# Seventh product on a copy in another bank, o's sums behind the gate, and the first two units side by side, in a fp32 decoder step

## The chip, the cores and the metric

The kernel runs on one core of a Trainium2 chip. The metric is device time in microseconds (us) for one execution; lower is better. The engines of a core work side by side and wait for one another through semaphores: TensorE (PE) multiplies matrices into PSUM banks, VectorE (DVE) and ScalarE (ACT) work on elements, GpSimd (POOL) does small work and starts stores, SyncE (SP) starts loads. Each engine runs its instructions in the order of its own queue.

## The reference

The program is one inference step of a decoder: 1024 prompt tokens and 8 decode tokens, model width 2048, everything in fp32. Two layers are computed, layer A (a pooling mixer) and layer B (sliding-window attention). Cut to the products:

```python
def pool_layer(x, ...):              # layer A
    z = x @ w_in                     # 2048 -> 4096
    u, gate = z[..., :D_POOL], z[..., D_POOL:]
    d, new_state = multiscale_pool(u, prefix, pos)   # windows 2, 4, 8, 16, minus u
    d = einsum('btgc,gce->btge', d, w_grp) * scale
    y = (d * silu(gate)) @ w_out
    return layer_norm(ALPHA * x + y, g_ln, b_ln), new_state

k, v = shared_kv(h)                  # 4 heads of 64, once, from layer A's output

def attn_layer(x, ...):              # layer B
    z = x @ w_in                     # 2048 -> 4096: queries and gate
    o = attn_core(rope(q), kb, vb)   # window of 128, a sink per head
    y = (o * silu(gate)) @ w_out
    return layer_norm(ALPHA * x + y, g_ln, b_ln)
```

The outputs are the result for prompt and decode tokens, and the new states of the pooling and of the keys and values.

## The kernel before

**Tokens and phases.** Chunk 0 holds 512 tokens; chunk 1 holds the other 512 and the 8 decode tokens, 520 columns. The program goes through ten phases in order: `ai` (input product of layer A) for chunk 0 in two parts and chunk 1, `ao` (output product of A) for chunks 0 and 1, `bi` (input product of B, with the attention beside it) for chunk 0 in two parts and chunk 1, `bo` (output product of B) for chunks 0 and 1. Activations and weights carry the letters x, g, h, o for the inputs of `ai`, `ao`, `bi`, `bo`, and `wia`, `woa`, `wib`, `wob` for the weights.

**An fp32 product from three.** Each weight tile and each activation tile is split into a high part, rounded to the matrix unit's format by a cast on ScalarE (L474 for weights, L752 for activations), and a low part, the rest, by a subtraction on VectorE (L489 and L761). For each of 8 slices of the inner dimension TensorE does three matmuls: high·high, high·low (the activation's low part), low·high (the weight's low part).

**Units and pairs.** The first part of `ai` and of `bi` is done in plain units (`unit`, L669 to L671): one 128 x 512 output from 16 slices, about 11.1 us. Everywhere else `pair` and `both` compute two output tiles at once by Strassen's scheme in Winograd's form (`seven`, L641 to L643): seven products of half the size, in the order 0, 2, 1, 5, 3, 4, 6 (another order for the first two pairs of most phases, which run interleaved in `both`). The products gather in PSUM banks a, b, c:

- product 0 goes to bank a; ScalarE writes its negative into bank b (`p0`, L582);
- product 2 goes to c, and is copied out (`p2`); product 1 is added in b, and copied out (`p1`);
- product 5 is added in a, and a is copied out (`p5`); product 3 is added in b, and VectorE subtracts product 2's copy from b into an output (`p3`, L602);
- product 4 is added in c, and VectorE subtracts from c (`p4`, L607); product 6 is added in b, and ScalarE copies b out (`p6`, L614).

The string that says this is `names = "abcbcab"`: the bank of product 0, 1, 2 and so on. Product 6 thus may start only when L602 has read b. With the `c11` and `split` forms a few pairs are treated in another way. Banks come from three pools (`psD`, a ring) and, in phases where `wide` holds, from four more (`psW`, used for a and c). A function such as `p3` is not issued at once: it is put into `posts`, and the next product's `begin` issues it first.

**Streams.** The weights come as a list of entries, in the order of use. `begin` (the start of each product) loads up to 7 entries ahead (SP, `load1`, L273), casts 4 ahead and makes low parts 3 ahead; in `bi` of chunk 1, where fewer than 4 whole slots are free, one less of each. The activations' tiles come in the same manner by `x_load`, `x_cast` and `x_make`. All of these live in 53 slots of on-chip memory (`NSLOT`); an entry whose slot is not free is loaded later. `end` (the end of each product) runs one late addition, the events that `at(n, go)` has put n products ahead, a step of the activations, and a step of the side work: generators such as `t_gen`, the layer norms, the sums of weights.

**Sums for Strassen's scheme.** Sums of weight quadrants are made once, on VectorE, and kept in DRAM: L279 in the first groups (four additions for each pair of rows, `late` in `plain_pair`, one at the end of each step), L332 and its neighbours later. Sums of activation quadrants are made by `t_ops` (four VectorE operations, L809 to L812), stored to `Td`, and loaded again by `x_load`; for x of chunk 0 `t_first` (L719 to L722) makes them from tiles still on chip.

**The attention of chunk 1 and o.** The attention runs beside the pairs of `bi`, tile by tile (t = 0 to 15): scores, exponentials (L1778), transposes, values, then `gate` (L1828), which writes a tile of o and stores it. For chunk 0 the sums of o are made right there from two neighbouring tiles (t − 1 and t). For chunk 1 the tile is freed at once; a side generator, `t_gen(("o", 1))`, added 18 steps into `bo` of chunk 0, later loads the pairs of tiles back (eight loads of 520 KB), sums them (eight calls of `t_ops`) and stores the sums. The decode tokens' own attention is done in small steps (L1919 to L1962) and stored into the last 8 columns of o.

**The start.** `start` issues the first loads, 512 KB each, in the order weight a, four tiles of x, weight, two of x, weight, two of x; then casts and low parts in the order of use. Unit 0 runs over all 16 slices, then unit 1 over the same tiles of x.

PE, VectorE and ScalarE keep the order of the source (`in_order`).

Of the kernel before, what the change touches and what calls it, by code (L numbers as in the profile page):

```python
# [9 lines left out]
F32 = mybir.dt.float32  # L10
# [52 lines left out]
ENGINES = (mybir.EngineType.PE, mybir.EngineType.DVE, mybir.EngineType.Activation)  # L63
NSLOT = 53
KEEP0 = 1

# [5 lines left out]

LATE = (2, 3)
X_KEEP = 5
X_AGE = 3
# [106 lines left out]
class Kern:  # L182
    def __init__(self, ctx, tc, io):
# [25 lines left out]
        self.ahead = 7, 4, 3  # L209
        dr = lambda n, s: dram.tile(s, F32, tag=n, name=n)  # L210
        self.Td, self.act, self.l_sq, self.l_sh = {}, {}, {}, {}
        for c, (_, T) in enumerate(CHUNKS):
# [56 lines left out]

    def load1(self, s, k, src):  # L270
# [15 lines left out]
    def plain_pair(self, name, q):  # L286

        a11, a12, a21, a22 = self.quads(name, q)
        ws = self.ws[name][q]
        s = {}  # L290
        ent = lambda k, src, after: Entry([self.load1(s, k, src)], [], lambda: s[k], after)
# [6 lines left out]
        return [  # L298
            ent("a", a11, []),
            ent("d", a12, []),  # L300
            ent("b", a21, []),
            ent("c", a22, [lambda: self.late.extend(late)]),
        ]

    def lone(self, src):
# [259 lines left out]
    def seven(self, c, z0, z1, after, c11=None, split=False, own=None):  # L565
# [4 lines left out]
        TH = T // 2  # L570
        B, o = {}, {}

        def out(i):
# [6 lines left out]
        def p0():  # L580
            B["b"] = self.psD()
            nc.scalar.mul(B["b"][:, :TH], B["a"][:, :TH], -1.0)  # L582
            if split:
                nc.scalar.copy(out(0)[:, :TH], B["a"][:, :TH])
# [15 lines left out]

        def p3():
            nc.vector.tensor_sub(out(1)[:, TH:T], B["b"][:, :TH], o["s"].a[:, :TH])  # L602
            if split:
                nc.scalar.copy(out(1)[:, :TH], B["b"][:, :TH])
# [5 lines left out]
        def p6():  # L610
            if split:
                nc.vector.tensor_add(out(1)[:, :TH], B["f"][:, :TH], out(1)[:, :TH])
            else:
                nc.scalar.copy(out(1)[:, :TH], B["b"][:, :TH])  # L614

        posts = {0: p0, 1: p1, 2: p2, 3: p3, 4: p4, 5: p5, 6: p6}
        names = "abcbcef" if split else "abcbcab"

        def run(idx):
# [11 lines left out]
            if new and own is not None and bank in "ac":  # L631
                B[bank] = own() if bank == "a" else B["a"]
            elif new:
                B[bank] = self.psW() if bank in "ac" else self.psD()
            ps = B[bank]
# [19 lines left out]
    def unit(self, done):  # L655
# [3 lines left out]
        for par in range(2):  # L659
            w = self.begin()  # L660
            wh, wl = (s.r for s in w)
            for k in range(8):
# [16 lines left out]
                if k in (3, 7):  # L679
                    self.end()  # L680


    def x_begin(self, n):
# [42 lines left out]
    def x_load(self):  # L726
        i, g = k = self.xl.pop(0)
        key = self.xkey
        T = CHUNKS[key[1]][1]
        TH = T // 2  # L730
        s = self.mem.full()
        if self.xseven:
            t = s.v(4, TH)
            if i in (0, 4, 5):
                k0, h = {0: (0, 0), 4: (1, 1), 5: (1, 0)}[i]
                src = self.act[key][:, 8 * g + k0 : 8 * g + 8 : 2, h * TH : (h + 1) * TH]
            else:
                src = self.Td[key][:, 4 * g : 4 * g + 4, {1: 0, 2: 1, 3: 2, 6: 3}[i], :]
        else:
            t = s.v(2, T)  # L740
            src = self.act[key][:, 4 * g + i : 4 * g + 4 : 2, :]
        self.nc.sync.dma_start(t, src)
        self.xraw[k] = s, self.i

    def x_cast(self, k):
        if k not in self.xraw:
            assert k == self.xl[0]
            self.x_load()
        s, _ = self.xraw.pop(k)
        n = 4 * (CHUNKS[self.xkey[1]][1] // 2) if self.xseven else 2 * TP  # L750
        h = self.mem.full()
        self.nc.scalar.copy(h.r[:, :n], s.a[:, :n])  # L752
        self.xhi[k] = s, h, n, self.i
# [361 lines left out]
    def phase_ai(self, c, gs, nxt):  # L1115
# [4 lines left out]
        for g in gs:  # L1120
            ext = es = None
            if T > TP:
                es = self.mem.half()
                ext = es.a[:, :512].rearrange("p (i b w) -> p i b w", i=4, b=NDEC)
                nc.sync.dma_start(ext, io["st"][:, 4 * g : 4 * g + 4])
            dd, sg = {}, {}
            for i in range(4):
                if not self.strassen:

                    def done(ps, i=i):  # L1130
                        U = self.mem.full()
                        nc.scalar.copy(U.a[:, NST : NST + T], ps[:])
                        self.at(1, lambda: self.pool_tile(c, 4 * g + i, U, None, dd))

                    self.unit(done)
                elif i % 2 == 0:
# [154 lines left out]
    def phase_end(self, c, xs, x_in, pre, acc, gc, bc, out):  # L1291
# [16 lines left out]
        A2 = slice(0, 2 * P)  # L1308
        four = self.small(NK * 4, 1)
        f3 = four[:].rearrange("p (k t) -> p k t", k=NK)  # L1310
        b2 = lambda x: x[:, None, :].to_broadcast([P, 2, TH])
# [416 lines left out]
    def attend(self, c, t, at, s1, s2, late=False):  # L1728
# [96 lines left out]
        def gate():  # L1825
# [6 lines left out]
            if c == 1:  # L1832
                self.ao.pop((c, t)).free(True)
            elif t % 2:
                e = self.ao.pop((c, t - 1))
                self.t_ops(e.a[:, :TP], a.a[:, :TP], self.Td["o", c], t // 2, T // 2)
                e.free(True)
                self.ao.pop((c, t)).free(True)
            if j == 1 or t == 15 or self.sg.get((c, t + 1), (None,))[0] is not z:
# [9 lines left out]
        self.product(at + s1 + s2, 1, values)  # L1849
        self.at(at + s1 + s2 + 1, gate)  # L1850

    def gate_done(self, c, t0, s, n):
# [29 lines left out]
    def decode(self, c, pr):  # L1882
# [77 lines left out]
        def s9():  # L1960
            a3 = self.sgd[pr][:]
            nc.vector.scalar_tensor_tensor(  # L1962
                a3, x["p"][:, :64].rearrange("p (b t) -> p t b", t=8), 0.5, a3,
                op0=ALU.mult, op1=ALU.mult,
            )
            nc.sync.dma_start(self.act["o", c][:, 8 * pr : 8 * pr + 8, TP:], a3)
            x["v"].free()
            W.free()
# [84 lines left out]
    def start(self):  # L2053
# [5 lines left out]
        self.x0, self.pre, self.held = {}, {}, set()  # L2059
        self.load_to(1)  # L2060
        for n in range(8):
            self.x_load()
            if n in (3, 5):
                self.load_to(n // 2 + 1)
# [3 lines left out]
        self.prep_to(1)  # L2068
        for n in range(8):
            self.x_make()  # L2070
            if n == 3:
                self.prep_to(2)
        for j in range(4):
# [7 lines left out]
    def run(self):  # L2081
# [15 lines left out]
        for n, (kind, c, part) in enumerate(PHASES):  # L2097
# [213 lines left out]
```

## Time and profile before

| | |
|---|---|
| median of 3 runs | 2367.22 us (2366.88 to 2370.61) |
| profiled execution | 2367.62 us |
| its span | 2365.9 us |
| TensorE busy | 2326.4 us, 98% |
| VectorE busy | 1923.5 us, 81% |
| ScalarE busy | 1342.2 us, 57% |
| GpSimd busy | 201.5 us, 9% |
| DMA | 669.18 MB, mean 283 GB/s |
| first matmul | 7.96 us after the span's start |

Times in rows count from the start of the span. The span covers the instructions; the execution's time has 1.7 us around it. A name before `<-` is what an instruction writes, those behind it are what it reads: `m` is a slot, `pD` a bank of PSUM of a product, `x1` the number of instructions. A bracket at the end of a row tells how long the engine had been idle before, and which instruction ended that. In a list of waits the line in front is the one that waited, the line behind the arrow the one that released it.

### The profile page before, as it was taken

How to read it: one execution, taken by the hardware profiler on the slowest of the kernel's cores; microseconds unless marked ns; L12 is line 12 of the kernel's file. 1: busy time of each engine (PE TensorE's matmuls, PEld its weight loads, DVE VectorE, ACT ScalarE, POOL GpSimd, SP SyncE). 2: the span in 40 equal slices, each digit the busy share in tenths (PEclk: the TensorE clock that was granted, in tenths of full speed). 3: DMA queues.
4: the chain of work that ended last, by engine and by line, in shares of the span. 5: the costliest groups of instructions: out<-in, count | busy, mean ns of one | idle time of the engine just before them, and what ended most of it. 6: DMA issues, size and time to landing. Idle time of an engine off the chain costs nothing. (4 is left out here: it accounts for less than half of the span.)

```text
span 2365.9 us, 46542 instructions
## 1 busy us (share of the span) xinstructions
PE 2326.4 (98%) x18424; PEld 2219.4 (94%) x18424; DVE 1923.5 (81%) x2385; ACT 1342.2 (57%) x2429; POOL 201.5 (9%) x379
## 2 busy tenths in 40 slices
PE   8999999999999999999999999999999999999997
PEld 6899999999999999998778899999999999999997
DVE  8787998776878878868888888887777768888887
ACT  4444446544536547554554656685666667546556
POOL 0111110001000000000111111100000000000000
PEclk9999999999999999999999999999999999999999
DMA  8678789889889989989888766788787768699785
GB/s 294 215 244 303 274 291 349 308 308 315 286 278 365 331 270 324 334 314 330 282 324 322 258 230 224 238 297 275 232 259 221 222 193 298 227 353 371 259 302 194
DMA packets 252059, 669.18 MB, mean 283 GB/s; under 512 B 25760, under 2 KB 106560, under 8 KB 251840
## 3 DMA queue, kind: packets, MB, share of 16 engines
q1 hardware_dynamic: 206368, 501.14, 64.0%
q0 software_dynamic: 45472, 165.07, 17.9%
q8 instruction: 144, 2.36, 0.4%
q14 instruction: 75, 0.61, 0.1%
HBM read 471.01 MB, written 185.59 MB: 278 GB/s over the span
## 5 line engine op out<-in xcount | busy, mean ns | idle before, releaser
L641 PE MATMUL pD<-m,m 128*128 128x260 f32 (+1 forms) x4752 | 1346.9, 283 | 9.9 <-DVE m L602 3.7
L643 PE MATMUL pD<-m,m 128*128 128x260 f32 (+1 forms) x4752 | 1340.5, 282 | 4.5 <-DVE m L489 4.5
L642 PE MATMUL pD<-m,m 128*128 128x260 f32 (+1 forms) x4752 | 1340.3, 282 | 0.0
L641 PEld LDWEIGHTS pD<-m,m 128*128 128x128 f32 x4752 | 896.0, 189 | 21.0 <-issue 10.2
L643 PEld LDWEIGHTS pD<-m,m 128*128 128x128 f32 x4752 | 896.7, 189 | 6.0 <-DVE m L489 6.0
L642 PEld LDWEIGHTS pD<-m,m 128*128 128x128 f32 x4752 | 896.3, 189 | 0.5
L489 DVE TENSOR_TENSOR m<-m,m 128x1024 fp32r<-128x1024 f32 x674 | 814.1, 1219 | 96.1 <-ACT m L474 58.3
L474 ACT CAST m<-m 128x1024 fp32r<-128x1024 f32 x674 | 701.6, 1048 | 305.2 <-DVE m L332 71.3
L669 PE MATMUL pD<-m,m 128*128 128x512 f32 x448 | 179.7, 401 | 8.0 <-ACT m L752 8.0
L670 PE MATMUL pD<-m,m 128*128 128x512 f32 x448 | 177.2, 396 | 0.5 <-DVE m L761 0.5
L671 PE MATMUL pD<-m,m 128*128 128x512 f32 x448 | 177.2, 396 | 0.0
L761 DVE TENSOR_TENSOR m<-m,m 128x1024 fp32r<-128x1024 f32 (+1 forms) x120 | 146.9, 1225 | 7.2 <-ACT m L752 5.7
L614 ACT COPY m<-pD 128x260 f32<-128x260 f32 (+1 forms) x83 | 31.0, 373 | 188.2 <-PE pD L643 188.1
L752 ACT CAST m<-m 128x1024 fp32r<-128x1024 f32 (+1 forms) x120 | 125.7, 1052 | 14.2 <-PE pD L670 5.2
L669 PEld LDWEIGHTS pD<-m,m 128*128 128x128 f32 x448 | 84.7, 189 | 29.9 <-ACT m L752 8.0
L332 DVE TENSOR_TENSOR m<-m,m 128x1024 f32<-128x1024 f32 x88 | 107.6, 1222 | 5.9 <-DMA m<-in_wia 4.2
L670 PEld LDWEIGHTS pD<-m,m 128*128 128x128 f32 x448 | 84.8, 189 | 20.4 <-DVE m L761 1.6
L671 PEld LDWEIGHTS pD<-m,m 128*128 128x128 f32 x448 | 84.6, 189 | 19.8
L602 DVE TENSOR_TENSOR m<-pD,m 128x260 f32<-128x260 f32 (+1 forms) x86 | 36.4, 424 | 81.9 <-PE pD L643 78.6
L1778 ACT ACTIVATE m<-m,sm 128x128 f32<-128x128 f32 x256 | 99.2, 390 | 0.0
L1071 PE MATMUL pD<-m,m 128*128 128x260 f32 (+1 forms) x528 | 91.5, 323 | 0.0
L607 DVE TENSOR_TENSOR m<-pD,m 128x260 f32<-128x260 f32 (+1 forms) x84 | 35.6, 424 | 64.2 <-PE pD L643 64.0
(243 smaller groups left out, 2167.3 us busy)
## 6 DMA issues: line engine op xcount, KB each, us to landing
m<-in_wia SPq DMA_DIRECT2D x124, 512.0 KB
m<-in_wib SPq DMA_DIRECT2D x120, 512.0 KB
swia<-m POOLq DMA_DIRECT2D x64, 512.0 KB, 4.9
m<-swia SPq DMA_DIRECT2D x64, 512.0 KB
m<-swoa SPq DMA_DIRECT2D x64, 512.0 KB
swib<-m POOLq DMA_DIRECT2D x64, 512.0 KB, 5.3
m<-swib SPq DMA_DIRECT2D x64, 512.0 KB
m<-swob SPq DMA_DIRECT2D x56, 512.0 KB
```

Source lines behind the costliest of these rows:

```text
L332: self.nc.vector.tensor_add(s[out].a[:, :1024], s[x].a[:, :1024], s[y].a[:, :1024])
L474: self.nc.scalar.copy(hi.r[:, :1024], self.stream[self.cast].src().a[:, :1024])
L489: self.nc.vector.tensor_sub(lo.r[:, :1024], s.src().a[:, :1024], hi.a[:, :1024])
L641: nc.tensor.matmul(ps[:, :TH], wh[:, s], h, start=new and k == 0, stop=False, skip_group_check=on)
L642: nc.tensor.matmul(ps[:, :TH], wh[:, s], l, start=False, stop=False, skip_group_check=on)
L643: nc.tensor.matmul(ps[:, :TH], wl[:, s], h, start=False, stop=k == 7, skip_group_check=on)
L669: nc.tensor.matmul(ps[:], wh[:, s], h, start=par == 0 and k == 0, stop=False)
L670: nc.tensor.matmul(ps[:], wh[:, s], l, start=False, stop=False)
L671: nc.tensor.matmul(ps[:], wl[:, s], h, start=False, stop=par == 1 and k == 7)
L752: self.nc.scalar.copy(h.r[:, :n], s.a[:, :n])
L761: self.nc.vector.tensor_sub(l.r[:, :n], s.a[:, :n], h.a[:, :n])
L1778: nc.scalar.activation(x["s3"][:, i, :], x["s3"][:, i, :], AF.Exp, bias=nm[:, i : i + 1], scale=0.125, accum_out=rs[:, i : i + 1],)
```

## The change

Three things are changed.

1. *Seventh product.* In pairs that are neither `split` nor the second of two interleaved ones (`turned`, 73 pairs), `p3` first copies bank b to bank a on ScalarE, from PSUM to PSUM; product 6 is added in a, and `p6` copies a out. VectorE's subtraction still reads b. Where the phase is not `wide`, a and b change places from pair to pair among the first two pools (`flip`), and c has the third.
2. *o's sums.* For chunk 1 the gate keeps the tiles of o; three steps after the gate of each odd t, `t_ops` sums tiles t − 1 and t over all 520 columns, with zeros in the decode columns. The decode tokens' columns are kept in a small tile (`oa`); `o_dec` sums them apart, once for each half of the heads, into `otd`, and `x_cast` puts them into the loaded tiles before the cast. The generator in `bo` is gone.
3. *The start.* Seventeen dummy matmuls on zeros are issued first. The first two weights and the first two tiles of x come in transfers of 256 KB with casts and subtractions of 512 columns. `first_units` runs unit 0 and unit 1 side by side, tile of x by tile of x, so that each tile feeds twelve matmuls; a few dummies are put between the first ones. The order of the first four weights is a, b, d, c. The small constants are loaded behind the fifth weight.

```diff
-            self.nc.sync.dma_start(s[k].a[:, :1024], src)
+            for a, b in cuts:
+                self.nc.sync.dma_start(s[k].a[:, a:b], src[:, a:b])
...
+        turned = own is None and not split
+        three = None
+        if turned and not self.wide:
+            self.flip = 1 - self.flip
+            three = {"a": self.flip, "b": 1 - self.flip, "c": 2}
...
         def p3():
+            if turned:
+                nc.scalar.copy(B["a"][:, :TH], B["b"][:, :TH])
             nc.vector.tensor_sub(out(1)[:, TH:T], B["b"][:, :TH], o["s"].a[:, :TH])
...
-                nc.scalar.copy(out(1)[:, :TH], B["b"][:, :TH])
+                nc.scalar.copy(out(1)[:, :TH], B["a" if turned else "b"][:, :TH])
...
-        names = "abcbcef" if split else "abcbcab"
+        names = "abcbcef" if split else "abcbcaa" if turned else "abcbcab"
...
+    def first_units(self, dones):
+        nc = self.nc
+        banks = [self.psD() for _ in dones]
+        for par in range(2):
+            ws = {}
+            for n, (u, j) in enumerate((u, j) for j in range(4) for u in range(2)):
...
+                for i in range(2):
+                    k = 2 * j + i
...
+                    nc.tensor.matmul(banks[u][:], wh[:, s], h, start=par == 0 and k == 0, stop=False)
+                    if par == 0 and n == 0:
+                        self.idle(FILL[i])
+                    nc.tensor.matmul(banks[u][:], wh[:, s], l, start=False, stop=False)
+                    nc.tensor.matmul(banks[u][:], wl[:, s], h, start=False, stop=par == 1 and k == 7)
...
             if c == 1:
-                self.ao.pop((c, t)).free(True)
-            elif t % 2:
+                nc.gpsimd.memset(a.a[:, TP:T], 0.0)
+                nc.gpsimd.tensor_copy(self.oa[:, t, :], a.a[:, THM - NDEC : THM])
+                self.o_dec(t // 8)
+            if t % 2:
                 e = self.ao.pop((c, t - 1))
...
+                def sums():
+                    self.t_ops(e.a[:, :T], a.a[:, :T], self.Td["o", c], t // 2, T // 2)
+                    e.free(True)
+                    self.ao.pop((c, t)).free(True)
...
+                if c == 1:
+                    self.at(3, sums)
+                else:
+                    sums()
...
+    def o_dec(self, pr):
...
+            nc.vector.tensor_sub(t[:, :, 1, :], Ea, Eb)
+            nc.vector.tensor_sub(t[:, :, 2, :], Eb, Ob)
+            nc.vector.tensor_add(t[:, :, 0, :], Ob, t[:, :, 1, :])
+            nc.vector.tensor_sub(t[:, :, 3, :], Oa, t[:, :, 0, :])
...
+        self.idle(WARM)
...
-                self.at(18, lambda: add(("o", 1, False), self.t_gen(("o", 1))))
```

More of the change, by code (lines that the diff above doesn't have):

```diff
@@ L290, in plain_pair @@
         s = {}
+        first = name == "wia" and q == 0
+        if first:
+            self.first_w = s
         ent = lambda k, src, after: Entry([self.load1(s, k, src)], [], lambda: s[k], after)
@@ L303, in plain_pair @@
         ]
+        return [e[0], e[2], e[1], e[3]] if first else e
     def lone(self, src):
@@ L571, in seven, with fresh @@
         B, o = {}, {}
+        turned = own is None and not split
[3 more added lines that the diff above has]
+            three = {"a": self.flip, "b": 1 - self.flip, "c": 2}
+        def fresh(bank):
+            if three is not None:
+                return self.psd[three[bank]].tile([P, 512], F32, tag="D", name=self.nm("pD"))
+            return self.psW() if bank in "ac" else self.psD()
         def out(i):
@@ L2067, in start @@
         nc.sync.dma_start(self.mki[:], io["mki"])
[L2068 to L2069 removed]
+        self.first_w.update(a=raw["a"], b=raw["b"])
+        self.hl[0], self.hl[1] = both["a"], both["b"]
+        self.cast = self.made = self.prepped = 2
+        for n, k in enumerate("xy"):
+            self.x0[0, n], self.xnew[0, n] = raw[k], both[k]
+        self.xq = self.xq[2:]
+        for it in plan:
+            if it is None:
+                self.x_make()
+                continue
+            k, lo, hi = it
+            h, l = both[k]
+            nc.scalar.copy(h.r[:, lo:hi], raw[k].a[:, lo:hi])
+            nc.vector.tensor_sub(l.r[:, lo:hi], raw[k].a[:, lo:hi], h.a[:, lo:hi])
+        for n in range(4, 8):
+            if n in (4, 5):
+                self.prep_to(n - 1)
             self.x_make()
[L2071 to L2072 removed]
         for j in range(4):
```

106 lines of the change are left out of this document (90 added, 16 removed).

## The prediction

> **What bounds the kernel now.** I read the shares per engine first, then the busy times by stretch, then TensorE's waits over the whole span, and then the instructions around those waits in order of time.
>
> ```profile
> span 2365.9 us, 46542 instructions
> PE 2326.4 (98%) x18424; PEld 2219.4 (94%) x18424; DVE 1923.5 (81%) x2385; ACT 1342.2 (57%) x2429; POOL 201.5 (9%) x379
> ```
>
> TensorE works for 98% of the span, so the change can win only out of 2365.9 − 2326.4 = 39.5 us of idle time, or out of time that TensorE spends at a lower clock.
>
> Busy time by stretch (columns: stretch, length, then PE, PEld, DVE, ACT and POOL busy with counts, granted clock, DMA share, GB/s):
>
> ```profile
> 0.00:20.00 20.00, 11.56 (x38) 8.63 (x39) 11.23 (x10) 11.99 (x12) 0.36 (x6) 1.00 0.93 336
> 20.00:60.00 40.00, 40.00 (x174) 32.36 (x173) 39.38 (x51) 15.92 (x25) 4.62 (x10) 1.00 0.75 271
> 2000.00:2300.00 300.00, 292.87 (x2516) 288.77 (x2515) 258.65 (x290) 178.18 (x266) 17.14 (x31) 1.00 0.88 306
> 2300.00:2365.90 65.90, 52.40 (x385) 48.83 (x383) 52.13 (x79) 40.63 (x76) 5.52 (x9) 0.92 0.55 195
> 1364.94:1368.35 3.41, 3.41 (x18) 3.41 (x18) 3.38 (x5) 0.90 (x1) 1.06 (x2) 0.50 0.55 225
> ```
>
> The first 20 us hold 8.4 us of the idle time and the last 66 hold 13.5; the change touches the first, not the last. Right behind, in 20 to 60 us, VectorE is busy for 39.38 of 40: whatever TensorE gains at the start runs into a VectorE that has nothing to spare. The last row is a stretch of 3.41 us at half clock.
>
> TensorE's waits over the whole span (waiting line, releaser, total, times, longest):
>
> ```profile
> PE pD L669 <- ACT m L752: 8.0, 1, 8.0
> PE pD L643 <- DVE m L489: 4.5, 7, 1.4
> PE pD L641 <- DVE m L602: 3.7, 4, 1.4
> PE pD L641 <- ACT pD L582: 3.6, 4, 1.9
> PE pD L641 <- ACT m L1778: 2.6, 1, 2.6
> ```
>
> The first is the start. The third is the wait that product 6 loses: it accumulates in the bank which L602 still reads. The second is VectorE being late with the low part of a weight; that one stays.
>
> **The start.** ScalarE, VectorE and TensorE in order of time (start, length, engine, line):
>
> ```profile
> 5.20 1.04 ACT L474 CAST m<-m 128x1024 fp32r<-128x1024 f32 x1 [3.19 <-DMA m<-in_wia]
> 6.86 1.04 ACT L752 CAST m<-m 128x1024 fp32r<-128x1024 f32 x1 [0.61 <-DMA m<-in_x]
> 7.96 0.79 PE L669 MATMUL pD<-m,m 128*128 128x512 f32 x1 [7.96 <-ACT m L752]
> 13.22 0.41 PE L670 MATMUL pD<-m,m 128*128 128x512 f32 x1
> 17.32 1.05 ACT L752 CAST m<-m 128x1024 fp32r<-128x1024 f32 x1 [1.53 <-DMA m<-in_x]
> 18.72 1.05 ACT L752 CAST m<-m 128x1024 fp32r<-128x1024 f32 x1 [0.35 <-DMA m<-in_x]
> 23.42 2.48 DVE L279 TENSOR_TENSOR m<-m,m 128x1024 f32<-128x1024 f32 x2
> 25.82 0.69 DVE L719 TENSOR_TENSOR m<-m 128x512 f32<-128x512 f32 x1
> 28.36 1.22 DVE L489 TENSOR_TENSOR m<-m,m 128x1024 fp32r<-128x1024 f32 x1
> 33.44 0.39 PE L669 MATMUL pD<-m,m 128*128 128x512 f32 x1
> ```
>
> Today 512 KB of weight lands at 5.20, the first tile of x is cast by 7.90, and the first matmul runs at 7.96. Unit 0 and unit 1 take 33.44 − 7.96 = 25.5 us, with slow matmuls up to about 13.2 (0.79 long, against 0.39 to 0.41 later).
>
> In halves, the first 256 KB should land about 0.65 us earlier (half of the 1.3 to 1.4 between the landings at 17.32 and 18.72), at 4.55; the half of x follows at 5.2, its cast takes 0.6, and the first real matmul stands at 5.9, a gain of 2.1. The 17 dummy matmuls run before that, while TensorE has nothing else; they cost nothing if they end by 5.9 (17 of 256 columns at half the slow spacing of 0.43, so 3.6 us, from about 1.3). The eight fill dummies cost up to 8 × 0.11 = 0.9. If the dummies raise the clock by 5.9, up to (13.22 − 7.96)/2 = 2.6 us of slow matmuls go as well. TensorE alone would then begin unit 2 between 29.0 and 30.5.
>
> VectorE does not allow that. The last tile of x is now the twelfth 512 KB; with 1.33 behind the landing at 18.72 it is there at 20.05, cast at 21.1, and its low part is made by 22.3. Behind it stand, in source order, the four additions of L279 (two take 2.4, so 4.8: to 27.1), one set of `t_first` (25.82 to 28.36, 2.5: to 29.6), and the low part of unit 2's weight (1.22: to 30.8). Unit 2's third matmul needs it, so its first is of use from 30.39. The gain is 33.44 − 30.39 = 3.05 us. The splitting costs VectorE little (0.6 for 512 columns against 1.14 for 1024), and the later units have low parts ready over 3 us ahead. Bounds: 1.5 if transfers of half the size run slower by a tenth (1.5 us over 20), 4.5 if VectorE catches up and the sum goes by TensorE alone.
>
> **Product 6 in the other bank.** The waits that go, with two rows for the spacing and VectorE's rows ahead of the longest:
>
> ```profile
> 609.50 0.28 PE L642 MATMUL pD<-m,m 128*128 128x260 f32 x1
> 609.61 0.28 PE L643 MATMUL pD<-m,m 128*128 128x260 f32 x1
> 610.92 0.36 PE L641 MATMUL pD<-m,m 128*128 128x260 f32 x1 [1.03 <-DVE m L602]
> 703.63 0.36 PE L641 MATMUL pD<-m,m 128*128 128x260 f32 x1 [0.32 <-DVE m L602]
> 1361.14 2.35 DVE L761 TENSOR_TENSOR m<-m,m 128x1024 fp32r<-128x1024 f32 x2
> 1363.41 0.42 DVE L602 TENSOR_TENSOR m<-pD,m 128x256 f32<-128x256 f32 x1
> 1363.98 0.36 PE L641 MATMUL pD<-m,m 128*128 128x256 f32 x1 [2.57 <-ACT m L1778]
> 2168.98 0.36 PE L641 MATMUL pD<-m,m 128*128 128x256 f32 x1 [0.99 <-DVE m L602]
> 2233.35 0.36 PE L641 MATMUL pD<-m,m 128*128 128x260 f32 x1 [1.38 <-DVE m L602]
> L582 ACT ACTIVATE pD<-pD x84: 358/368/372, 114.3 to 2302.7; 128x260 f32<-128x260 f32 x49, 128x256 f32<-128x256 f32 x35
> ```
>
> A matmul is 0.28 long and the next starts 0.12 after it, so each loses its idle time and 0.16: 1.19, 0.48, 1.15 and 1.54, together 4.36. At 1363.98 the list of waits names L1778, but L602 ends at 1363.83 and the matmul starts 0.15 behind it, as in the other four: it is the same wait. Of its 2.73 only a part can go: the two L761 in front make product 6's low parts of the activations, the first of them done at about 1362.36, and the second matmul reads it. So product 6 starts at about 1362.3 and gains 1.65. The sum is 6.0.
>
> Behind that wait the clock drops to 0.50 for 3.41 us (the stretch above), which costs at most half of it, 1.7. With 1.1 us of idle time left in place of 2.57 I let the drop go and count 1.5. The sum of this part is −7.5.
>
> What is added is an ACT copy between two banks in 73 pairs, as long as L582's (0.37): 27 us on an engine that is busy for 57%. It stands at the head of ScalarE's queue after product 3 and waits for it; the casts of weights stand behind it. I laid each pair's copy at the later of product 3's end and ScalarE's previous operation's end: in 72 of the 73 it ends 1.0 us or more ahead of product 6, in one, near 2146, with it. No cast behind a copy moves the low part of a weight by more than 0.1. So the copy costs nothing; product 4 (2.9 us) covers it. Without cover the price is L582's, which is waited for in the same way: 3.6 us in 84, so 3.1 in 73. Bounds of this part: −9 (the wait at 1363.98 wholly gone) and −7.5 + 1.5 + 3.1 = −3.
>
> **The sums of o behind the gate.**
>
> ```profile
> 2065.26 0.39 PE L643 MATMUL pD<-m,m 128*128 128x256 f32 x1 [0.25 <-DVE m L489]
> 2072.53 0.38 PE L643 MATMUL pD<-m,m 128*128 128x256 f32 x1 [1.35 <-DVE m L489]
> 2063.65:2076.00 12.35, 10.75 (x89) 10.34 (x88) 12.28 (x14) 5.34 (x8) 2.12 (x4) 1.00 0.93 316
> 2130.81 0.42 DVE L809 TENSOR_TENSOR m<-m 128x260 f32<-128x260 f32 x1
> 2131.94 0.43 DVE L812 TENSOR_TENSOR m<-m,m 128x260 f32<-128x260 f32 x1
> ```
>
> Eight sets of four VectorE operations, 2131.94 + 0.37 − 2130.81 = 1.5 us each, leave 2085 to 2132, with eight loads of 520 KB on SP. No wait of TensorE lies in that stretch, and the low parts there are ready 2 us or more ahead: the gain is nothing. Six sets go into the first three quarters of the attention of chunk 1, where low parts are mostly ready over 3 us ahead, and one beside product 626, ready 2.2 ahead: nothing. The last, with the four small operations of the decode tokens (four times 0.12, about 0.5; 1.4 if each took as long as a wide one), stands just before the low part of product 638, and there VectorE is the bound: it works for 12.28 of 12.35, and TensorE waits for it at 2065.26 and 2072.53. All 1.5 + 0.5 = 2.0 us come on the path: +2.0. GpSimd's 16 memsets and 16 copies of 8 columns stand behind the gate's own stores, and nothing on TensorE waits for them. The o halves are held longer, so about ten more products of this phase look ahead by 5 loads in place of 6: nothing, for 5 products are some 15 us. Bounds: 0 (the wait at 2072.53 swallows it) and +5 (two more products of the phase late by 1.5).
>
> **The sum**: −3.05 − 7.5 + 2.0 = −8.55, from the profiled execution's 2367.62 to 2359.1. That execution lies 0.4 above the median of the runs, 2367.22.
>
> **A rule beside the rows.** The Trainium skill, "TensorE: Matmul & The Clock Gate", Part 1: The HAM clock gate, says that activity over a window of some 3.4 us releases a default half clock, and that an idle window brings it back; the window runs freely, so the cold time differs from run to run. The trace agrees on the length, 3.41, and on the cold start. It differs on the drop: 2.57 us of idle time, less than one window, were enough. By the rule the drop at 1364.94 need not hang on this wait, and the third rival below is that case.
>
> **The rivals.**
>
> *The lateness moves (0.18).* VectorE's stream is the same as before, and TensorE, ahead of it, waits for L489 where it waited for L602. For it: 39.38 of 40 us at the start, and VectorE's full 12.28 of 12.35 near the end. Against it: after each of the four L602 waits the next low part is ready over 1.4 us ahead. The start gives 1.5, the waits at 2168.98 and 2233.35 give nothing (2.7 less), the sums cost 2: 2367.62 − 1.5 − 4.8 + 2.0 = 2363.3.
>
> *Slower: the attention of chunk 1 runs out of slots (0.09).* Loads have no time to landing in the list of DMA issues; the nearest row is a store of the same size:
>
> ```profile
> swia<-m POOLq DMA_DIRECT2D x64, 512.0 KB, 4.9
> ```
>
> The held o halves take the slots into which weights are loaded. A load of 4.9 with a cast (1.05) and a low part (1.22) makes 7.2 us; a product lasts 2.9. With two products of lookahead or more the path is hardly touched; with one, each of the six pairs loses 4.3, 26 us: 2367.6 − 10.5 + 2 + 26 = 2385. It decides from a lookahead of one on; against it, 5 stand in the program.
>
> *The clock falls anyway (0.10).* The half-clock stretch comes with another gap: 1.5 more, 2360.6.
>
> *The start does not do what it says (0.08).* The dummies raise no clock and TensorE runs slow until 9 or 10: 5.9 + 22.2 + 2.0 + 0.9 = 31.0 for unit 2, half a us behind VectorE's bound: 2359.7, and 2362.1 if transfers in halves bring nothing at all (unit 2 at 33.44).
>
> **How the numbers follow.** The forecast has 0.55, the rivals 0.45. From no change the measurement can tell 0.2%, 4.7 us. Forecast, clock and start lie below 2362.5 (0.73 together); of the first rival and what is unforeseen most counts as no change: 0.16; slower: 0.11. The range goes from 2355.5 (start by TensorE alone, sums hidden) to 2366.5 (bank −3, start −1.5, sums +3.4).
>
> **What would show it.** Product 6 has no wait for L602 left in its 73 pairs; an added wait of L641 for the copy in p3 would prove the bank wrong. The first product matmul stands near 5.9, unit 2 near 30.4, with a wait for L489 in front. Between 2060 and 2070 a wait for L489 grows by 2. No load of o's pairs after 2085. Wrong would be the forecast if waits for L489 or L474 appear in 1700 to 2000, or if 1364 keeps its wait.

## The result and the profile after

| | before | after |
|---|---|---|
| median | 2368.41 us (5 runs) | 2387.32 us (5 runs) |
| profiled execution, span | 2367.62, 2365.9 us | 2387.48, 2385.7 us |
| ratio | | 1.0082, 95% interval 1.0071 to 1.0094 |

The change makes the kernel slower by 18.9 us, where 8.5 us less were forecast. The first lines of the changed kernel's page, and two groups of its instructions (busy, mean ns of one, idle time in front and what ended most of it):

```profile
span 2385.7 us, 46732 instructions
PE 2335.2 (98%) x18449; PEld 2227.5 (93%) x18449; DVE 1925.4 (81%) x2398; ACT 1367.8 (57%) x2514; POOL 207.4 (9%) x411
...
L626 DVE TENSOR_TENSOR m<-pD,m 128x260 f32<-128x260 f32 (+1 forms) x86 | 36.6, 425 | 112.4 <-ACT pD L625 105.9
```

TensorE is idle for 50.5 us (2385.7 − 2335.2), 11 more than before, and busy for 8.8 us longer although it has only 25 dummies more: some of its work ran at a lower clock. TensorE's waits over the whole span:

```profile
PE pD L665 <- ACT m L613: 18.3, 4, 8.3
PE pD L667 <- DVE m L501: 6.4, 7, 2.4
PE pD L665 <- ACT pD L604: 5.9, 6, 1.9
PE pS L1818 <- DVE m L1790: 2.3, 4, 1.5
PE pD L710 <- DVE m L2165: 1.3, 1, 1.3
PE pD L695 <- DVE m L501: 1.2, 1, 1.2
```

In the changed file L665 to L667 are the product matmuls (L641 to L643 before), L501 makes low parts (L489), L604 is `p0` (L582), L613 is `p1`, L625 the new copy between banks, L626 VectorE's subtraction (L602). The wait of 8.0 at the start and TensorE's waits for L602 are gone. A new one stands on top: four waits for `p1`, 18.3 us. All lie in the attention of chunk 1. The same stretch, before and then after (columns as in the prediction):

```profile
1700.00:1960.00 260.00, 259.15 (x2364) 250.12 (x2363) 182.56 (x242) 168.77 (x406) 13.98 (x22) 1.00 0.70 220
```

```profile
1700.00:1960.00 260.00, 240.21 (x2100) 231.32 (x2100) 173.90 (x247) 153.17 (x373) 18.17 (x43) 0.95 0.65 207
1835.92:1839.33 3.41, 3.41 (x15) 3.41 (x16) 2.33 (x4) 3.34 (x8) 0.00 (x0) 0.50 0.22 90
```

Before, TensorE is busy for 259 of these 260 us; after, for 240, and at 0.95 of the clock: a stretch of half clock like the one in the last row follows each of the four waits. VectorE and ScalarE are *less* busy than before, in part because fewer products fit into the 260 us. They do not work harder; something holds them.

To see where time goes, the 602 products of `seven` (86 pairs of seven) can be matched one to one by their order; the times are those of the kernel before. At 111 us the changed kernel is 2.0 us ahead, at 1369 it is 8.3 ahead, at 1498 5.4, at 1934 it is 22.8 behind, at 2068 24.9 behind, at the end 19.7. Up to 1369 the forecast was 7.9 (3.05 + 1.19 + 0.48 + 1.65 + 1.5). Of the 8.3, however, 1.5 come from a stretch of half clock at 361 that the profile before shows and this one does not, and that comes and goes between executions (see "The clock" below). So the start and the bank bring somewhat less than forecast. The 28 us are lost between 1700 and 1934, and 2.1 more at 2068.

The longest wait, in order of time (VectorE, GpSimd, ScalarE, TensorE):

```profile
1718.76 1.22 DVE L501 TENSOR_TENSOR m<-m,m 128x1024 fp32r<-128x1024 f32 x1 [7.26 <-DMA to<-m]
1721.39 0.58 PE L665 MATMUL pD<-m,m 128*128 128x260 f32 x1 [3.90 <-ACT m L613]
...
1822.08 0.43 DVE L881 TENSOR_TENSOR m<-m,m 128x260 f32<-128x260 f32 x1
1822.81 0.55 POOL L882 DMA_DIRECT2D to<-m  x1 [11.39 <-DVE m L881]
1832.21 1.04 ACT L486 CAST m<-m 128x1024 fp32r<-128x1024 f32 x1 [9.79 <-issue]
1835.50 0.37 ACT L613 COPY m<-pD 128x260 f32<-128x260 f32 x1
1835.92 0.59 PE L665 MATMUL pD<-m,m 128*128 128x260 f32 x1 [8.28 <-ACT m L613]
...
1890.40 1.04 ACT L486 CAST m<-m 128x1024 fp32r<-128x1024 f32 x1 [6.60 <-DMA to<-m]
1894.11 0.39 PE L665 MATMUL pD<-m,m 128*128 128x260 f32 x1 [4.10 <-ACT m L613]
...
1945.77 1.22 DVE L501 TENSOR_TENSOR m<-m,m 128x1024 fp32r<-128x1024 f32 x1 [5.42 <-DMA to<-m]
1948.40 0.39 PE L665 MATMUL pD<-m,m 128*128 128x260 f32 x1 [2.06 <-ACT m L613]
```

L881 is the last operation of a set of o's sums, L882 its store, `to<-m`. In three of the four a cast or a low part waits for that store to end. Such a cast *writes* a slot; the slot it was given is the one from which the sums are still being stored. ScalarE works in order: behind the waiting cast stands `p1`, the copy out of bank b, and TensorE's product 3 waits for `p1`. Where a low part on VectorE is the one that waits, ScalarE's next cast waits for VectorE (8.4 us at 1720, 6.6 at 1947), and `p1` stands behind it again. At 1832.21 the view names no releaser, but the trace holds the landing of each store: 1718.57, 1832.14, 1890.24 and 1945.58. Each of the four writers starts 0.07 to 0.19 us behind one of these. The list of DMA issues has the median from issue to landing:

```profile
to<-m POOLq DMA_DIRECT2D x8, 520.0 KB, 6.0
```

In the attention of chunk 1 a store of this size took 3.2 to 9.3 us. The slots are given out when the program is built: the allocator takes the one that was freed longest ago, counts a slot that is being stored from (`free(True)`) as freed ten releases later, and cannot know when a store will have landed. Followed through the build, the changed kernel gives out a slot with a store just issued after one product at products 543, 571, 585 and 599 for a cast or a low part; the four waits come two products behind each. In the kernel before, no cast and no low part waits for a store in this stretch. SyncE's weight loads do, for up to 6.3 us at a time, and TensorE does not feel it: they run further ahead (up to 6 entries here) than casts (3) and low parts (2).

### The profile page after: what moved, and what is told of

It reads as the page before. It is cut to its first block, busy times and chain, and to the rows that moved or that the text cites. A ratio compares the mean times of both kernels' runs of the same rounds, so it can differ in the third digit from the quotient of the medians.

```text
span 2385.7 us, 46732 instructions
## 1 busy us (share of the span) xinstructions
PE 2335.2 (98%) x18449; PEld 2227.5 (93%) x18449; DVE 1925.4 (81%) x2398; ACT 1367.8 (57%) x2514; POOL 207.4 (9%) x411
## 3 DMA queue, kind: packets, MB, share of 16 engines
q8 instruction: 144, 2.36, 0.4%
## 5 line engine op out<-in xcount | busy, mean ns | idle before, releaser
L665 PE MATMUL pD<-m,m 128*128 128x260 f32 (+1 forms) x4752 | 1349.2, 284 | 24.4 <-ACT m L613 18.3
L667 PE MATMUL pD<-m,m 128*128 128x260 f32 (+1 forms) x4752 | 1342.1, 282 | 6.4 <-DVE m L501 6.4
L665 PEld LDWEIGHTS pD<-m,m 128*128 128x128 f32 x4752 | 898.1, 189 | 36.0 <-ACT m L613 19.2
L667 PEld LDWEIGHTS pD<-m,m 128*128 128x128 f32 x4752 | 898.7, 189 | 8.1 <-DVE m L501 8.1
L666 PEld LDWEIGHTS pD<-m,m 128*128 128x128 f32 x4752 | 898.4, 189 | 1.3 <-DVE m L830 0.8
L501 DVE TENSOR_TENSOR m<-m,m 128x1024 fp32r<-128x1024 f32 x672 | 811.7, 1220 | 107.6 <-ACT m L486 61.3
L693 PE MATMUL pD<-m,m 128*128 128x512 f32 x416 | 165.9, 399 | 0.0
L695 PE MATMUL pD<-m,m 128*128 128x512 f32 x416 | 163.7, 394 | 1.2 <-DVE m L501 1.2
L694 PE MATMUL pD<-m,m 128*128 128x512 f32 x416 | 163.8, 394 | 0.0
L626 DVE TENSOR_TENSOR m<-pD,m 128x260 f32<-128x260 f32 (+1 forms) x86 | 36.6, 425 | 112.4 <-ACT pD L625 105.9
L693 PEld LDWEIGHTS pD<-m,m 128*128 128x128 f32 x416 | 78.1, 188 | 20.5 <-issue 3.2
L695 PEld LDWEIGHTS pD<-m,m 128*128 128x128 f32 x416 | 78.1, 188 | 19.9 <-DVE m L501 1.7
L694 PEld LDWEIGHTS pD<-m,m 128*128 128x128 f32 x416 | 78.1, 188 | 17.2
L1140 PEld LDWEIGHTS pD<-m,m 128*128 128x128 f32 x528 | 79.4, 188 | 8.2
```

The lines of the kernel that those rows point to most:

```text
L501: self.nc.vector.tensor_sub(lo.r[:, :1024], s.src().a[:, :1024], hi.a[:, :1024])
L665: nc.tensor.matmul(ps[:, :TH], wh[:, s], h, start=new and k == 0, stop=False, skip_group_check=on)
L666: nc.tensor.matmul(ps[:, :TH], wh[:, s], l, start=False, stop=False, skip_group_check=on)
L667: nc.tensor.matmul(ps[:, :TH], wl[:, s], h, start=False, stop=k == 7, skip_group_check=on)
L693: nc.tensor.matmul(ps[:], wh[:, s], h, start=par == 0 and k == 0, stop=False)
L694: nc.tensor.matmul(ps[:], wh[:, s], l, start=False, stop=False)
```

## The experiments

**Which part.** First the sums of o alone undone (`gate`, `o_dec` and `t_gen` as before), and alone done:

```diff
-                if c == 1:
-                    self.at(3, sums)
...
+            if c == 1:
+                self.ao.pop((c, t)).free(True)
```

> The changed kernel with the sums of o as they were before (o's tiles of chunk 1 freed at the gate, the side generator in the output product of chunk 0); the start and the bank of product 6 stay changed. Theory A (the held tiles of o take the slots into which weights are loaded in the attention of chunk 1), theory B (not the held tiles, but the slot of each set of sums, which is given out again while its store is under way), theory C (GpSimd's added memsets and copies hold up its stores): all three lie in what is undone here, so 2357 to 2361. Theory D (the copy between banks holds up ScalarE's queue in the attention of chunk 1): still 2380 or more, with waits of TensorE for ScalarE between 1700 and 1960.

Measured: 2368.53 us against 2367.48 before, ratio 1.0004 (0.9993 to 1.0014).

> The kernel before with the sums of o behind the gate alone. A, B, C: the whole loss without the gains, about 2368 + 28 = 2396 (2388 to 2402), with waits for ScalarE of 2 to 8 us between 1700 and 1960. D: 2366 to 2372.

Measured: 2389.53 us against 2367.48, with these waits between 1700 and 1960:

```profile
PE pD L665 <- ACT m L613: 16.5, 4, 7.4
PE pS L1812 <- DVE m L1784: 1.6, 4, 0.6
PE pD L665 <- ACT pD L604: 0.4, 1, 0.4
```

The run with the sums of o alone, like the others below that stand without a ratio, is a single execution. The loss lies in the sums of o: alone they bring the same four waits, with neither the start nor the bank changed. D falls: without them, 1700 to 1960 holds one wait of 0.9. But the first run missed its number: start and bank were to give 2357 to 2361, and gave nothing. A second loss must lie there; it is taken up below.

**Held tiles, or the sums' own slot.**

```diff
+    def drop():                          # tiles held, no sums
+        e.free(True)
+        self.ao.pop((c, t)).free(True)
+    self.at(3, drop)
...
+    def sums():                          # sums of the odd tile alone
+        self.t_ops(a.a[:, :T], a.a[:, :T], self.Td["o", c], t // 2, T // 2)
+        self.ao.pop((c, t)).free(True)
+    self.at(3, sums)
```

> The kernel before, where the tiles of o of chunk 1 are kept until three products after the gate of each odd one, and then freed; no sums are made there and nothing else is changed. A: 2385 to 2400. B, C, D: 2366 to 2371.

Measured: 2368.09 us against 2367.48. A falls as a cause by itself: holding the tiles alone costs nothing.

> The kernel before with eight sets of sums three products behind the gate of each odd tile, made from that tile alone and stored (the generator in the output product then writes the right sums over them); the even tiles are freed at once. A: under 2375. B: 2380 to 2400. C, D: 2366 to 2372, and at most 2 more for VectorE's added work.

Measured: 2381.82 us, 14 more than before. That is B's range. The sums of o as they are in the changed kernel cost 22 (2389.53), so some 7 us more come from what this run and the one before it leave out, or from held tiles and sums together; no run separates these.

> The kernel before with the eight sets of sums made from the odd tile alone three products behind the gate, as in the run with the sums alone, but not stored (the generator in the output product makes and stores the right ones). It takes the same slots at the same places, and the same work of VectorE; no slot waits for a store. B: 2367 to 2371. If VectorE's work or the number of slots is the cause: 2378 to 2385.

The right sums are still made and stored by the generator. Measured: 2374.03 us against 2368.12, between the two expectations. Its waits between 1700 and 1960:

```profile
PE pD L641 <- ACT pD L582: 2.8, 2, 1.9
PE pS L1743 <- DVE m L1715: 1.7, 3, 1.1
PE pD L643 <- DVE m L489: 0.3, 1, 0.3
```

So of the 14 us some 8 hang on the store; the other 6 come without it, from VectorE's work or the slot that it takes, which this run does not separate. B is right about the larger part, not the whole.

**Taking the cause away.** Sums written over the two tiles, so that no slot is added:

```diff
+    nc.vector.tensor_sub(Ea, Ea, Eb)
+    nc.vector.tensor_sub(Eb, Eb, Ob)
+    nc.vector.tensor_add(Ob, Ob, Ea)
+    nc.vector.tensor_sub(Oa, Oa, Ob)
+    nc.gpsimd.dma_start(d[:, 1:3], ...)      # and two more for rows 3 and 0
```

> The changed kernel, where o's sums for chunk 1 are written over the two tiles that they are made from and stored from there in three transfers, so that no further slot is taken; the held tiles, VectorE's operations and GpSimd's memsets and copies stay. B (the slot of each set of sums, given out again while its store is under way): most of the 28 us between 1700 and 1960 go, 2358 to 2366. If the two tiles' own stores take the part of the sums' slot: 2375 or more. C (GpSimd's queue), E (the planner's order of SyncE's queue in this phase, whatever the slots): 2383 or more.

Measured: 2379.70 us, ratio 1.0049 (1.0034 to 1.0064). The second branch came: the two tiles' own stores take the part of the slot's. The longest wait stands there again, now on a slot of the tiles (stores land at 1823.41 and 1827.04):

```profile
1823.51 0.38 ACT L610 COPY m<-pD 128x260 f32<-128x260 f32 x1 [4.61 <-DMA to<-m]
...
1827.12 2.54 DVE L501 TENSOR_TENSOR m<-m,m 128x1024 fp32r<-128x1024 f32 x2 [6.68 <-DMA to<-m]
```

What counts is thus not how many slots are taken but whether the next one to be given out has a store under way. Two runs change only that:

```diff
-                    e.free(True)
-                    self.ao.pop((c, t)).free(True)
+                    e.free(c == 0)
+                    self.ao.pop((c, t)).free(c == 0)
```

> The changed kernel, where the two tiles of o are given back as slots at once free of stores (their stores are three products old), so that the allocator takes them before the slot of the sums; nothing else. In the changed kernel a slot with a store under way is given out again one product later at products 543, 571, 585 and 599 (for a cast or a low part), and TensorE's four waits of 2 to 8 us stand two products behind these. Here it happens at 557 and 571 alone. B (the reused slot): the losses at 545, 587 and 601 go, 4.1 + 2.8 - 1.0 + 4.3 + 2.0 + 2.2 + 2.0 = 16 us, 2371 (2366 to 2376), the wait at 573 stays. If VectorE's and ScalarE's load in this phase is the cause: 2385 or more.

Measured: 2373.07 us, ratio 1.0023 (1.0013 to 1.0032). 14 us are gone by two flags in the allocator's book-keeping; each engine has as many instructions as before the edit, they stand in other slots. The steps at 545, 587 and 601 are gone, one of 1.9 us stands behind 557, and the long one at 573 stays:

```profile
PE pD L667 <- DVE m L501: 7.2, 1, 7.2
PE pS L1818 <- DVE m L1790: 2.8, 3, 1.8
PE pD L665 <- ACT pD L604: 0.4, 1, 0.4
```

The second run has this edit too, and one more place where slots are taken, the side work that sums wob:

```diff
-                if m < len(parts) and (not held and (self.on and len(self.mem.whole()) > 5 or hurry)):
+                if m < len(parts) and (not held and (self.on and len(self.mem.whole()) > 7 or hurry)):
```

> As the run before it, and the side work that sums wob in the attention of chunk 1 starts a part only with more than 7 whole slots free (5 before). No slot with a store under way is given out one product later in this phase or the next. B: the wait at 573 goes as well, 2358 to 2365. If the sums' work itself costs 6 us, as the run without their store had it, 2364 to 2368.

Measured: 2366.34 us, ratio 0.9994 (0.9984 to 1.0003), 21 less than the changed kernel. All that is left between 1700 and 1960, and then from 1960 to 2120:

```profile
PE pS L1818 <- DVE m L1790: 0.8, 1, 0.8
...
PE pD L667 <- DVE m L501: 6.7, 6, 2.4
PE pS L1895 <- DVE m L1881: 0.7, 1, 0.7
PE pO L667 <- DVE m L501: 0.5, 1, 0.5
```

The attention of chunk 1 is clean, with the sums still made there: B holds for the loss in this phase. The total came 1 us above B's range and inside that of the other branch, by which the sums' work costs some 6 us. The cost shows later: in the output product, where VectorE is the bound, waits for L501 grow (2.5 between 2040 and 2085 before, and none ahead of that in this phase). That it is the side work held back from the attention, now done there, is argued and not shown. The GpSimd theory C needs no run of its own: its memsets, copies and order were in these two runs too. E was not tested by itself; what waits in this phase are writers of slots and not loads that came in another order.

**Why start and bank alone gave nothing.** In the run without the sums the lead of 6.6 us at 1369 shrinks to 3.7 at 1498, and at 2137 one step takes 7.8 us. Around it, in that run (GpSimd, SyncE, VectorE):

```profile
2118.66 0.53 POOL L876 DMA_DIRECT2D to<-m  x1 [6.63 <-DVE m L875]
...
2125.27 0.38 SPq L885 DMA_DIRECT2D m<-o  x1
...
2132.88 0.43 DVE L872 TENSOR_TENSOR m<-m 128x260 f32<-128x260 f32 x1 [5.62 <-DMA m<-o]
```

In the kernel before the last two loads of o's generator were issued together:

```profile
2117.14 3.01 SPq L822 DMA_DIRECT2D m<-o  x2
```

The order of SyncE's queue is not that of the source: a planner lays it when the program is built. With the changed start it puts the eighth load of o five places further back, sixth behind the seventh load of o instead of next to it, behind loads of weights that wait for slots (the expectation below says seven places; the traces of both runs with this start show five). One of these waits is the long one (SyncE's waits in the run without the sums, 2117 to 2127):

```profile
SPq L278 <- DMA to<-m: 4.6, 1, 4.6
```

It is the same thing again. A weight is to be loaded into a slot from which a set of sums is being stored, the store issued at 2118.66 in the rows above; it lands at 2124.35, that weight's load starts at 2124.36, and the load of o stands behind it. VectorE then waits 5.6 us for o, and the low part behind it is late.

> The kernel before with the new start alone. The start gives -2.0. Here the eighth load of o's generator stands seven places later on SyncE's queue than before, as it did in the run without the sums: F expects +7.8 at 2137, so 2368 - 2 + 7 = 2373 (2371 to 2376). G expects 2366.

Measured: 2372.62 us against 2368.12, ratio 1.0022 (1.0012 to 1.0031).

> The kernel before with product 6 in the other bank alone. The traces so far price this part at about -6 up to 1370 us, +2.7 at two products of the first chunk's attention (1448 and 1498), and -4 behind 2150: 2368 - 7 = 2361 (2359 to 2363). The eight loads of o's generator stand on SyncE's queue in the order they had before, so theory F (a load of o's generator, moved behind weight loads by the planner that orders SyncE's queue, cost the 7.8 us at 2137 in the run without the sums) expects nothing at 2137 here. The other view, G (the copy between banks holds up ScalarE at 2137), expects the 7.8 us here: 2369.

Measured: 2367.54 us, ratio 0.9997 (0.9988 to 1.0007). F has both signs right: the step at 2137 comes with the start (8.3 us), whose queue is turned and where SyncE's weight load waits 5.6 us for the store, and is absent with the bank, whose queue is not turned. G falls at 2137. But the bank's own gain missed its range by 4.5 us. Its waits, 1440 to 1500 and 2140 to 2150:

```profile
PE pD L662 <- ACT pD L601: 2.4, 2, 1.2
...
PE pD L662 <- ACT pD L622: 2.3, 1, 2.3
```

Here L601 is `p0` and L622 the copy between banks. Twice TensorE comes to product 1 earlier than before and waits for `p0`, which stands behind exponentials that have not come forward as far (at 1446 TensorE is 3.4 us ahead, `p0` 1.8); once the copy itself is late, behind a cast whose weight was late to land. In the trace 5.1 us of the gains go back at these three places, and the rest in steps under 0.8.

Last, start and bank with o's generator one product earlier, first together, then the start alone:

```diff
-                self.at(18, lambda: add(("o", 1, False), self.t_gen(("o", 1))))
+                self.at(17, lambda: add(("o", 1, False), self.t_gen(("o", 1))))
```

> The changed start and bank with o's sums in the side generator, as in the run without the sums behind the gate, but the generator is added 17 steps into the output product of chunk 0 and not 18. Its eighth load stands four places behind the seventh on SyncE's queue (six in that run, one in the kernel before). F (the place of that load): the 7.8 us at 2137 shrink or go, 2361 to 2365. If it is the generator's work on VectorE that comes late there: 2368 or more.

Measured: 2361.28 us against 2367.52, ratio 0.9973 (0.9962 to 0.9984): faster than both kernels. The eighth load is issued at 2116.19, none of SyncE's loads around it waits for a store, and the step at 2137 is gone. The edit moves the whole generator by one product and not this load alone, so the order of the queue and the time of the sums are not separated.

> The kernel before with the new start alone, and o's generator added 17 steps into the output product of chunk 0, its loads in the same order as in the run with start, bank and that generator (2361.3). If the bank gives back what it gains (the run with the bank alone: 0.6 less than before), the start carries that run: 2361 to 2364. If the bank is worth its four waits once the loss at 2137 is away: 2365 to 2367.

Measured: 2367.19 us against 2368.39, ratio 0.9995 (0.9985 to 1.0004). It is the second branch. With the bank the gain over the kernel before was 6.2 us by the medians, without it 1.2, so the bank is worth some 5 us here, where alone it was worth 0.6. The profiled executions, 2365.1 and 2366.4, differ by 1.3 only, and the first is the slowest run of its kernel. It has a half clock at 361 (1.5 us) that the other has not, and at 732 a wait of 2.0 for `p0`, where the run without the sums, the same program up to there, waits 1.0 and is 1.8 us quicker over that step; that makes up most of the difference. One reason why the bank pays in this company and not alone is in the traces: the 2.5 us that it loses at 2148 alone are not lost here. The rest stays open.

## Why the prediction was wrong

**The sums of o: the step that failed.** "Six sets go into the first three quarters of the attention of chunk 1 … nothing": 28 us were lost there. The step looked at when low parts were ready (over 3 us ahead) and asked nothing else of VectorE's work. What it left out is the sums' store: 520 KB, 3.2 to 9.3 us to land in this stretch, from a slot that a phase with few free slots gives out again one product, 2.9 us, later. The prediction counted the loads that go away in the later phase and names the sums' stores nowhere, though a step that is moved takes its stores with it. The step beside it, "The o halves are held longer … nothing", held by itself: the run that only holds them lost 0.6 us. Its sign of being wrong, waits for L489 or L474 in 1700 to 2000, came in disguise: the late cast stands in front of `p1`, and TensorE's wait carries the name of `p1`.

**The slower rival.** It had the right phase and the right scarcity, and the wrong mechanism: it waited for loads with a lookahead of one product. Loads were early enough: between 1700 and 1960 the longest wait of a cast or low part for a load is 1.7 us. That its number, 2385, lies near the measured 2387 is luck: it adds six losses of 4.3, where four of 4 to 11 came, clock included.

**The last set of sums.** +2.0 at product 638 was forecast; the step there is 2.1. The gain at 2085 to 2132, put at nothing, was nothing against the kernel before, but with the new start the generator would have come late, as the runs that keep it show: 8 us that the changed kernel never pays.

**The start.** −3.05 was forecast, −2.0 measured at 111 us. The mechanism holds: first real matmul at 5.75 (forecast 5.9), clock up soon after, unit 2 waiting for its weight's low part. In the changed kernel:

```profile
5.75 0.79 PE L729 MATMUL pD<-m,m 128*128 128x512 f32 x1 [0.43 <-ACT m L2211]
...
7.18 0.39 PE L732 MATMUL pD<-m,m 128*128 128x512 f32 x1
...
20.70 1.06 ACT L821 CAST m<-m 128x1024 fp32r<-128x1024 f32 x1 [0.21 <-DMA m<-in_x]
...
30.48 2.35 DVE L501 TENSOR_TENSOR m<-m,m 128x1024 fp32r<-128x1024 f32 x2
31.75 0.50 PE L695 MATMUL pD<-m,m 128*128 128x512 f32 x1 [1.25 <-DVE m L501]
```

The mis-sized term is the transfers: the last tile of x came at 20.7, not 20.05, which is 0.65 of the 0.9 by which the low part was late (31.7, not 30.8); VectorE's work between the two took the rest.

**The bank.** TensorE's waits for L602 went as forecast: 1.2 and 0.5 at 611 and 704, 1.5 at 2233, and 2.5 + 0.6 at 1364 and behind it, where the half clock was gone too (2.7 + 0.4 with the bank alone; 3.15 counted). At 2169, 2.4 came where 1.15 was counted, but the two runs with the start and without the bank gain 2.1 and 1.2 there, so not all of it is the bank's. What failed is that the sum kept the whole lead: at 1448 and 1498 2.7 us of it go back, in every run with the bank and in none without. "So the copy costs nothing" held in the changed kernel, where no wait of TensorE names L625. With the bank alone it failed once, by 2.3 at 2148: this is the pair near 2146 for which the prediction had the copy end together with product 6, and no cost was put on it. Two things in the traces were not in the prediction. First, VectorE's subtraction now waits for ScalarE: L626's idle time is 112 us, 106 of it ended by L625, where L602 had 81.9, nearly all ended by TensorE. The Trainium skill, "PSUM — Partial Sum Buffer", in Terms, says that two engines must not be in the same bank at once, reads against reads included; the order L625, L626 in the trace agrees with it, and no run here lets the two overlap. Second, the lead brings TensorE to `p0` before ScalarE, which is where the 2.7 go back: the rival "the lateness moves" was right in kind, with L604 in the place of L489 (5.9 us of waits, 3.6 before).

**The clock.** The drop behind 1364 is in none of the seven profiles with the changed bank, where 1.1 us of idle time or less is left. Of the seven that keep the wait of 2.6 us, six have the drop and one, that of o's sums alone, has not. So the 1.5 counted for it is what most executions lose and not all. The drop at 361 behaves in the same way: gone in the changed kernel's profile, there in that of the bank alone, 1.5 us either way. And four new drops came with the four new waits.

## What to carry to other kernels

Before moving a store, ask which buffer it leaves from and when the allocator will hand that buffer out again; in a phase with few free buffers a store's 6 us are a wait for whoever writes there next, and an engine or a queue that works in order spreads it to all that stands behind. It did so twice here, once through ScalarE and once through SyncE's queue of loads. A side effect of the book-keeping (here which slot is given out, and where a planner puts one load) can cost more than the work that was changed: two flags were worth 14 us, one load five places later 8. And a wait that is taken away is worth its length only as far as the next engine is early: follow the lead to the next place where it can be given back.

## What the runs showed of the hardware

A store of 520 KB from GpSimd's queue took 3.2 to 9.3 us to land in the attention of chunk 1 (median of the eight 6.0), and the next writer of its slot started 0.07 to 0.19 us behind the landing.

TensorE's clock fell to half behind the four new waits, idle times of 2.06 to 8.28 us, for 3.4 us or two or three times that; where it fell, a wait of 2 us cost nearly as much again in clock. But it did not always fall. The two rows are from the changed kernel, the first behind the shortest of the four, the second behind an idle time of 2.36 us:

```profile
1948.40:1951.90 3.50, 3.50 (x19) 3.50 (x20) 2.42 (x3) 3.43 (x8) 0.00 (x0) 0.63 0.03 7
2090.10:2093.50 3.40, 3.38 (x28) 3.38 (x29) 3.40 (x4) 1.43 (x2) 0.53 (x1) 1.00 0.59 240
```

The granted clock is 0.63 in the first and 1.00 in the second. An idle time of 1.9 us near 360 was followed by a drop in six of the fourteen profiles and not in eight, and one of 3.11 us at 1886, in the run with sums in place, was not. Idle times up to 1.5 us were followed by none, between 30 and 2290 us. The Trainium skill, "TensorE: Matmul & The Clock Gate", Part 1: The HAM clock gate, gives one idle window of about 3.4 us as what brings the half clock back; here idle times from 1.9 us on were at times enough, and the measurement decides.
